# Feed-forward up products with both parts of the rows as one moving operand of 512 columns

## Chip, cores and metric

The kernel runs on one core of a Trainium2 chip. The metric is the device time of one execution in microseconds, lower is better. The engines are TensorE (PE in the profile; its weight loads are PEld), VectorE (DVE), ScalarE (ACT), GpSimd (POOL) and SyncE (SP), which issues the loads from HBM.

## What is computed

Two layers of a decoder trunk over 256 rows of 1024 features. Each layer has an attention part and a feed-forward part. Only the second changes:

```python
def conv_ffn(h, w_up, conv_w, conv_b, w_down):
    u = h @ w_up
    s = u.shape[1]
    up = jnp.pad(u, ((0, 0), (CONV_WIDTH - 1, 0), (0, 0)))
    c = conv_b
    for k in range(CONV_WIDTH):
        c = c + conv_w[k] * up[:, k:k + s]
    a, val = jnp.split(c, 2, axis=-1)
    return (jax.nn.gelu(a, approximate=True) * val) @ w_down
```

Here h is 256 x 1024 (the normalised rows), w_up is 1024 x 5632, the convolution runs over three neighbouring rows, and w_down is 2816 x 1024.

## The kernel before

All products are made from two parts of each operand, for precision: a high part that TensorE's fast 32-bit format holds exactly (`copy` on ScalarE rounds to it, L113) and a low part, the difference (`sub` on VectorE, L116). A product is then three matmuls: high by high, high by low, low by high (`mm3`, L375). Weights come through a stream (`Stream`, L145): each chunk of 512 KB is loaded into one of four `st` buffers, its high part is written into one of four `wh` buffers and its low part into one of four `wl` buffers. A chunk is requested two chunks ahead of its use (`next`, L198).

A scheduler orders the instructions of each engine from the program and a model of their times; every engine then runs its own queue in that order and waits on semaphores. A pool tag with several buffers is given out as they come free. PSUM has eight banks of 512 32-bit columns, two for each of the tags T, mm, S and O (`bank`, L92); accesses to one bank are kept in program order.

The feed-forward stage is `ffn_layer` (L992). The rows stand transposed in two tiles of 128 partitions x 8 slices x 256 rows: `hh` (high part) and `hl` (low part), tag `q8`, written by `t8` (L388) from `out_layer` (L950). There are 22 column groups j of 128 features, each with two halves (the gelu side and the value side):

- j = 0 and 1: `up_first` (L1055) makes them with the rows as stationary operand and 512 weight columns as moving one, and `up_first_T` (L1072) transposes the result into T banks.
- j = 2 to 21: `up(j, half)` (L1014) has the weights as stationary operand and the rows as moving one. For each of the 8 slices k there are three matmuls of 256 columns: `wh` with `hh` (L1022), `wh` with `hl` (L1023), `wl` with `hh` (L1024). All 24 accumulate into the same 256 columns of a bank; the two halves of a j lie side by side in one bank. The banks go T, T, mm, mm over four j.
- `act_gate(j, half)` (L1028), called after both halves: `conv` (L1004) reads the bank three times (ScalarE L1007, VectorE L1008 and L1009); then come the gelu (L1031), the product of the two halves (L1035) and its split into `gh` and `gl`.
- `down(j, t)` (L1041): `mm3` on two banks of 512 columns, 12 matmuls for both t. It runs two groups behind: a round is up of j (both halves), then down of j - 2. The last two j have their up products one after the other; eight down steps follow in a fixed order.

After the last down products of a row half, `post_norm` and, in layer 0, `gained` and `t8` make the rows for the next layer. Queries (`qA`, `qB`, `qR`, L549) and the branch outputs (`out_T`, L698) of the attention part use the same tag `q8`, three buffers of 8 KB per partition, and so does the first chunk of the up weights. The 128-column rows, the convolution results and `gh`, `gl` are tiles of tag `k1`, eleven buffers.

Of the kernel before, what the change touches and what calls it, by code (L numbers as in the profile page):

```python
# [16 lines left out]
P = 128  # L17
# [48 lines left out]
def tile_hybrid_trunk(  # L66
# [138 lines left out]
    TAGS = {"kB": 1, "sg": 2, "q8": 3}  # L205
# [225 lines left out]
    def attn_layer(l, xp, rs, gains, first):  # L431
# [117 lines left out]
        qA, qB, qR = big8("q8", 3), big8("q8", 3), big8("q8", 3)  # L549
# [148 lines left out]
        def out_T(br, g):  # L698
            if OT[br] is None:
                OT[br] = big8("q8", 3)  # L700
            bv = OB[br][g].rearrange("p (k c) -> p k c", k=2)
            ho = OT[br][:, g * 2:g * 2 + 2, :]
            copy(ho, bv)
            sub(OT[br][:, 4 + g * 2:6 + g * 2, :], bv, r32(ho))
# [243 lines left out]
        return yp  # L948

    def out_layer(l, yp, gains):  # L950
        gains["ffn_pre"] = gain_tile(ffn_pre_gain, l)
        res = [[bank("O"), bank("O")], [bank("S"), bank("S")]]
        hp = big8("q8", 3), big8("q8", 3)
# [35 lines left out]
        return hp  # L989


    def ffn_layer(l, hp, gains, last):  # L992
        hh, hl = hp
# [10 lines left out]
        def conv(b, jj, half):  # L1004
            c = k1()
            u = b[:, half * T:(half + 1) * T]
            act.activation(c, u, AF.Identity, bias=cb(l, jj), scale=cw(l, 2, jj))  # L1007
            dve.scalar_tensor_tensor(c[:, 1:T], u[:, 0:T - 1], cw(l, 1, jj), c[:, 1:T], ALU.mult, ALU.add)  # L1008
            dve.scalar_tensor_tensor(c[:, 2:T], u[:, 0:T - 2], cw(l, 0, jj), c[:, 2:T], ALU.mult, ALU.add)  # L1009
            return c  # L1010
# [3 lines left out]
        def up(j, half, c0, c1):  # L1014
            if j not in up_bank:
                up_bank[j] = bank("T" if j % 4 < 2 else "mm")
# [3 lines left out]
            o = up_bank[j][:, half * T + c0:half * T + c1]  # L1020
            for k in range(8):
                pe.matmul(o, wh[:, k, :], hh[:, k, c0:c1], start=(k == 0), stop=False, skip_group_check=True)  # L1022
                pe.matmul(o, wh[:, k, :], hl[:, k, c0:c1], start=False, stop=False, skip_group_check=True)  # L1023
                pe.matmul(o, wl[:, k, :], hh[:, k, c0:c1], start=False, stop=(k == 7), skip_group_check=True)  # L1024
# [3 lines left out]
        def act_gate(j, half):  # L1028
            if half == 0:
                ca = ga[j] = conv(up_bank[j], j, 0)  # L1030
# [3 lines left out]
            cv = conv(up_bank.pop(j), 22 + j, 1)  # L1034
# [52 lines left out]
        for j in range(2, NJ):  # L1087
            for half in range(2):
                part(lambda: up(j, half, 0, T))
# [96 lines left out]
    for l in range(DEPTH):  # L1186
        yp = attn_layer(l, xp, rs, gains, l == 0)
        hp = out_layer(l, yp, gains)
        xp, rs = ffn_layer(l, hp, gains, l == DEPTH - 1)
# [79 lines left out]
```

## Time and profile before

| | us |
|---|---|
| median of three runs | 783.96 |
| lowest, highest | 782.5, 784.26 |
| the profiled execution | 782.81 |
| its span, first to last instruction | 781.0 |

In a profile, busy time is that in which an engine had an instruction under way. Matmuls overlap: the duration shown for one is longer than the distance to the next, so their rate is read from start to start. Idle time is put down to what released the engine, as inferred from semaphores. Names in rows leave out buffer numbers: `q` is any tile of tag `q8`, `k` any tile of tag `k1`, `k2` or `k4`; `mm`, `T`, `S` and `O` are banks.

### The profile page before, as it was taken

The numbers are of one execution on the slowest core, as the hardware profiler recorded it, in microseconds if no ns is written. First come the engines' busy times: TensorE is split into PE (matmuls) and PEld (weight loads), VectorE is DVE, ScalarE is ACT, GpSimd is POOL, SyncE is SP. The second block draws the span as 40 slices with busy tenths as digits, with TensorE's granted clock in tenths as the row PEclk, the third lists the DMA queues.
The fourth block names the chain that finished last, engine by engine and source line by source line (L and its number), as shares of the span: only waits on it lengthen the run. The fifth ranks groups of instructions, "written<-read, shape, count | busy, mean of one in ns | idle before, by whom it ended". The sixth has DMA issues, their size and how long they took to land.

```text
span 781.0 us, 12886 instructions
## 1 busy us (share of the span) xinstructions
PE 759.2 (97%) x4742; PEld 676.8 (87%) x4742; DVE 613.1 (79%) x1188; ACT 495.4 (63%) x950; POOL 34.0 (4%) x60
## 2 busy tenths in 40 slices
PE   8999999999899999999989999999999999999996
PEld 6788898887799999999868889988878999999995
DVE  6899898686787777777787989985876877677775
ACT  6596986754665555565556969866465655566552
POOL 4300001000100000000010000010010000000000
PEclk9999999999999999999999999999999999999999
DMA  8624264465566565665545323644645556656731
GB/s 337 196 86 133 64 219 170 136 188 162 173 205 189 188 187 184 209 210 188 164 134 163 95 82 121 200 153 162 200 144 172 188 187 189 188 182 201 217 104 54
DMA packets 42346, 131.26 MB, mean 168 GB/s; under 512 B 5375, under 2 KB 5931, under 8 KB 42283
## 3 DMA queue, kind: packets, MB, share of 16 engines
q1 hardware_dynamic: 41707, 129.39, 52.0%
q10 hardware_dynamic: 576, 1.05, 0.4%
q8 instruction: 37, 0.61, 0.3%
q14 instruction: 26, 0.21, 0.1%
HBM read 129.37 MB, written 1.05 MB: 167 GB/s over the span
## 4 chain that ended last, share of the span: by engine, by line
PE 83%; ACT 8%; DVE 4%; POOL 2%; issue 1%; DMA 1%; SPq 0%; DVEq 0%; POOLq 0%; ACTq 0%
PE mm L376 6%; PE mm L378 6%; PE mm L377 6%; PE T L1024 5%; PE mm L1023 5%; PE T L1023 5%; PE mm L1024 5%; PE T L1022 5%; PE mm L1022 5%; PE S L377 5%; PE S L376 5%; PE S L378 5%; PE O L376 3%; PE O L377 3%; PE O L378 3%; ACT k L635 2%
## 5 line engine op out<-in xcount | busy, mean ns | idle before, releaser
L117 DVE TENSOR_TENSOR wl<-st,wh 128x1024 fp32r<-128x1024 f32 (+2 forms) x220 | 260.4, 1186 | 101.5 <-ACT wh L114 100.3
L114 ACT ACTIVATE wh<-st 128x1024 fp32r<-128x1024 f32 (+2 forms) x220 | 225.5, 1028 | 178.1 <-PE O L378 40.5
L376 PE MATMUL mm<-wh,x 128*128 128x512 f32 (+2 forms) x248 | 92.9, 375 | 0.7 <-DVE VT L546 0.6
L377 PE MATMUL mm<-wl,x 128*128 128x512 f32 (+2 forms) x248 | 91.6, 370 | 0.0
L378 PE MATMUL mm<-wh,x 128*128 128x512 f32 (+2 forms) x248 | 91.3, 368 | 0.1
L1023 PE MATMUL mm<-q,wh 128*128 128x256 f32 x320 | 90.7, 284 | 0.0
L1024 PE MATMUL T<-q,wl 128*128 128x256 f32 x320 | 90.6, 283 | 0.0
L1023 PE MATMUL T<-q,wh 128*128 128x256 f32 x320 | 90.6, 283 | 0.0
L1024 PE MATMUL mm<-q,wl 128*128 128x256 f32 x320 | 90.6, 283 | 0.0
L1022 PE MATMUL T<-q,wh 128*128 128x256 f32 x320 | 90.5, 283 | 0.0
L1022 PE MATMUL mm<-q,wh 128*128 128x256 f32 x320 | 90.5, 283 | 0.0
L1022 PEld LDWEIGHTS mm<-q,wh 128*128 128x128 f32 x320 | 61.4, 192 | 0.9
L1022 PEld LDWEIGHTS T<-q,wh 128*128 128x128 f32 x320 | 61.4, 192 | 0.8
L1023 PEld LDWEIGHTS mm<-q,wh 128*128 128x128 f32 x320 | 61.4, 192 | 0.8
L1023 PEld LDWEIGHTS T<-q,wh 128*128 128x128 f32 x320 | 61.4, 192 | 0.7
L1024 PEld LDWEIGHTS mm<-q,wl 128*128 128x128 f32 x320 | 61.4, 192 | 0.1
L1024 PEld LDWEIGHTS T<-q,wl 128*128 128x128 f32 x320 | 61.4, 192 | 0.0
L378 PEld LDWEIGHTS mm<-wh,x 128*128 128x128 f32 x248 | 46.7, 188 | 6.1 <-DVE x L117 0.5
L376 PEld LDWEIGHTS mm<-wh,x 128*128 128x128 f32 x248 | 46.7, 188 | 6.0 <-issue 0.8
L377 PEld LDWEIGHTS mm<-wl,x 128*128 128x128 f32 x248 | 46.7, 188 | 4.8
L635 ACT ACTIVATE k<-k,mn 128x128 f32<-128x128 f32 (+1 forms) x96 | 42.4, 445 | 7.1 <-DVE mn L632 7.0
L114 ACT ACTIVATE k<-k 128x256 fp32r<-128x256 f32 x72 | 29.1, 413 | 9.1 <-DVE k L1035 5.6
(294 smaller groups left out, 1657.0 us busy)
## 6 DMA issues: line engine op xcount, KB each, us to landing
st<-in_ffn_w_up_dram SPq DMA_DIRECT2D x88, 512.0 KB, 4.2
st<-in_ffn_w_down_dram SPq DMA_DIRECT2D x44, 512.0 KB, 3.9
st<-in_w_in_dram SPq DMA_DIRECT2D x42, 512.0 KB, 3.6
st<-in_w_out_dram SPq DMA_DIRECT2D x16, 512.0 KB, 3.8
st<-in_w_in_dram SPq DMA_DIRECT2D x16, 384.0 KB, 3.1
st<-in_cmp_w_dram SPq DMA_DIRECT2D x16, 256.0 KB, 2.6
st<-in_w_branch_a_dram SPq DMA_DIRECT2D x8, 512.0 KB, 3.6
st<-in_w_branch_b_dram SPq DMA_DIRECT2D x8, 512.0 KB, 3.5
```

The costliest lines, as they stand in the source:

```text
L114: return act.activation(dst, src, AF.Copy, scale=scale)
L117: dve.tensor_tensor(dst, a, b, ALU.subtract)
L376: pe.matmul(o, xh, wh, start=first, stop=False, skip_group_check=True)
L377: pe.matmul(o, xh, wl, start=False, stop=False, skip_group_check=True)
L378: pe.matmul(o, xl, wh, start=False, stop=last, skip_group_check=True)
L635: last_exp[0] = act.activation(self.pt[:, hh, s, :], sm[:, :nk], AF.Exp, bias=self.mn[:, i:i + 1], scale=-1.0, accum_out=self.dn[:, i:i + 1])
L1022: pe.matmul(o, wh[:, k, :], hh[:, k, c0:c1], start=(k == 0), stop=False, skip_group_check=True)
L1023: pe.matmul(o, wh[:, k, :], hl[:, k, c0:c1], start=False, stop=False, skip_group_check=True)
L1024: pe.matmul(o, wl[:, k, :], hh[:, k, c0:c1], start=False, stop=(k == 7), skip_group_check=True)
```

## The change

The two parts of the rows now lie in one tile `H` of 128 partitions x 2 parts x 8 slices x 256 rows (tag `h16`, one buffer of 16 KB per partition). `H[:, 0]` and `H[:, 1]` serve in turn as `qA` and `qB`, as the branch outputs, and as `hh` and `hl`; tag `q8` keeps one buffer, for `qR` and the first chunk of the up weights.

For j from 2 on, a slice k is two matmuls: `wh` with both parts of the rows as one moving operand of 512 columns, which fills a whole bank (left half: with the high part, right half: with the low part), and `wl` with the high part, 256 columns, added to the left half. Each half of a j has a bank of its own, mm for even j and T for odd j. Before the convolution, `left` copies the right half of the bank to SBUF on ScalarE and adds the left half on VectorE; the convolution then reads the sum from SBUF. The first two j are as before.

```diff
-    TAGS = {"kB": 1, "sg": 2, "q8": 3}
+    TAGS = {"kB": 1, "sg": 2, "q8": 1}
...
-        qA, qB, qR = big8("q8", 3), big8("q8", 3), big8("q8", 3)
+
+        H = ap_.tile([P, 2, KD, T], F32R, tag="h16", name=nm("H"))
+        qA, qB, qR = H[:, 0], H[:, 1], big8("q8", 1)
...
-                OT[br] = big8("q8", 3)
+                OT[br] = H[:, br]
...
-        hp = big8("q8", 3), big8("q8", 3)
+        hp = H[:, 0], H[:, 1]
...
-        def conv(b, jj, half):
+        def conv(u, l_, jj):
             c = k1()
-            u = b[:, half * T:(half + 1) * T]
...
-        def up(j, half, c0, c1):
-            if j not in up_bank:
-                up_bank[j] = bank("T" if j % 4 < 2 else "mm")
+
+        def up(j, half):
+            b = up_bank[j, half] = bank("mm" if j % 2 == 0 else "T")
             if (j, half) not in up_w:
                 up_w[j, half] = W.next(8, P)
             wh, wl, _ = up_w[j, half]
-            o = up_bank[j][:, half * T + c0:half * T + c1]
+            both = b.rearrange("p (s t) -> p s t", s=2)
             for k in range(8):
-                pe.matmul(o, wh[:, k, :], hh[:, k, c0:c1], start=(k == 0), stop=False, skip_group_check=True)
-                pe.matmul(o, wh[:, k, :], hl[:, k, c0:c1], start=False, stop=False, skip_group_check=True)
-                pe.matmul(o, wl[:, k, :], hh[:, k, c0:c1], start=False, stop=(k == 7), skip_group_check=True)
+                pe.matmul(both, wh[:, k, :], H[:, :, k, :], start=(k == 0), stop=False, skip_group_check=True)
+                pe.matmul(b[:, 0:T], wl[:, k, :], hh[:, k, :], start=False, stop=(k == 7), skip_group_check=True)
+
+        def left(j, half):
+            if j < 2:
+                return up_bank[j][:, half * T:(half + 1) * T]
+            b = up_bank.pop((j, half))
+            u = k1()
+            copy(u, b[:, T:2 * T])
+            dve.tensor_tensor(u, b[:, 0:T], u, ALU.add)
+            return u
...
-                ca = ga[j] = conv(up_bank[j], j, 0)
+                ca = ga[j] = conv(left(j, 0), l, j)
...
-            cv = conv(up_bank.pop(j), 22 + j, 1)
+            cv = conv(left(j, 1), l, 22 + j)
```

## Rows read from the trace of the kernel before

**Rows 1.** The page: busy us, share of the span, instructions of each engine.
```profile
PE 759.2 (97%) x4742; PEld 676.8 (87%) x4742; DVE 613.1 (79%) x1188; ACT 495.4 (63%) x950; POOL 34.0 (4%) x60
```
**Rows 2.** Busy us by stretch; columns as in the first line.
```profile
core 0: us, PE busy (x) PEld busy (x) DVE busy (x) ACT busy (x) POOL busy (x), PEclk, DMA share, GB/s
...
239.26:358.64 119.38, 119.38 (x842) 112.14 (x840) 88.72 (x129) 68.06 (x100) 0.00 (x0) 1.00 0.62 195
...
624.00:743.38 119.38, 119.38 (x842) 112.14 (x840) 88.74 (x129) 68.29 (x100) 0.00 (x0) 1.00 0.63 194
```
**Rows 3.** Longest of PE's waits from 206 to 400: total us, times, longest.
```profile
PE T L383 <- DVE k L415: 2.9, 2, 1.6
```
**Rows 4.** PE in order of time, one round: start us, duration us, line, operation.
```profile
281.90 0.28 PE L1022 MATMUL mm<-q,wh 128*128 128x256 f32 x1
...
287.53 0.28 PE L1024 MATMUL mm<-q,wl 128*128 128x256 f32 x1
287.65 0.39 PE L376 MATMUL S<-wh,k 128*128 128x512 f32 x1
...
290.42 0.28 PE L1022 MATMUL mm<-q,wh 128*128 128x256 f32 x1
```
**Rows 5.** PE in time: third input tile (41 us), first up products (200 us).
```profile
41.53 0.40 PE L376 MATMUL mm<-wh,x 128*128 128x512 f32 x1
...
43.13 0.39 PE L377 MATMUL mm<-wl,x 128*128 128x512 f32 x1
...
200.72 0.39 PE L376 MATMUL mm<-wh,q 128*128 128x512 f32 x1
...
204.58 0.39 PE L378 MATMUL mm<-wh,q 128*128 128x512 f32 x1
```
**Rows 6.** PE in time: eight matmuls of 32 columns, and the next.
```profile
133.41 0.96 PE L825 MATMUL S<-kcs,q 128*128 128x32 f32 x8
134.22 0.48 PE L376 MATMUL mm<-wh,x 128*128 128x512 f32 x1
```
**Rows 7.** Groups from 239.26 to 358.64: busy us, mean ns | idle before, releaser.
```profile
L117 DVE TENSOR_TENSOR wl<-st,wh 128x1024 fp32r<-128x1024 f32 x42 | 51.4, 1224 | 25.0 <-ACT wh L114 24.8
L1008 DVE SCALAR_TENSOR_TENSOR k<-T,vec,k 128x255 f32<-128x255 f32 x16 | 7.6, 477 | 0.0
L1035 DVE TENSOR_TENSOR k<-k,k 128x256 f32<-128x256 f32 x14 | 6.0, 425 | 0.5
...
L114 ACT ACTIVATE wh<-st 128x1024 fp32r<-128x1024 f32 x42 | 44.2, 1058 | 43.4 <-PE O L378 16.3 <-PE T L1023 13.7 <-PE mm L1023 13.4
```
**Rows 8.** Groups by form, whole execution, columns as above.
```profile
L114 ACT ACTIVATE k<-mm,rstd 128x256 f32<-128x256 f32 x8 | 3.3, 467 | 0.0
L407 DVE SCALAR_TENSOR_TENSOR X<-k,rstd,X 128x512 f32<-128x512 f32 x16 | 11.4, 747 | 1.7 <-POOL rstd L365 1.7
L490 DVE SCALAR_TENSOR_TENSOR k<-mm,rstd,tab 128x512 f32<-128x512 f32 x4 | 3.0, 747 | 1.6 <-POOL tab L358 1.6
```
**Rows 9.** ACT and DVE in time: a weight chunk's two parts, with idle time before.
```profile
279.20 1.06 ACT L114 ACTIVATE wh<-st 128x1024 fp32r<-128x1024 f32 x1 [1.49 <-PE T L1023]
...
280.30 1.23 DVE L117 TENSOR_TENSOR wl<-st,wh 128x1024 fp32r<-128x1024 f32 x1 [1.32 <-ACT wh L114]
```
**Rows 10.** DVE and PE in time: last read of a T bank, second half of j = 3.
```profile
224.43 0.48 DVE L1009 SCALAR_TENSOR_TENSOR k<-T,vec,k 128x254 f32<-128x254 f32 x1
...
226.52 0.28 PE L1022 MATMUL mm<-q,wh 128*128 128x256 f32 x1
```
**Rows 11.** In time, end of layer 0's stage: last up matmul, convolutions, low part.
```profile
378.56 0.28 PE L1024 MATMUL T<-q,wl 128*128 128x256 f32 x1
...
380.03 0.55 ACT L1007 ACTIVATE k<-T,vec 128x256 f32<-128x256 f32 x1
...
382.74 0.55 ACT L1007 ACTIVATE k<-T,vec 128x256 f32<-128x256 f32 x1
...
386.68 0.42 DVE L117 TENSOR_TENSOR k<-k,k 128x256 fp32r<-128x256 f32 x1
```

More of the change, by code (lines that the diff above doesn't have):

```diff
@@ L947, in attn_layer, with out_layer @@
         branch(1)
-        return yp
-    def out_layer(l, yp, gains):
+        return yp, H
+    def out_layer(l, yp, H, gains):
         gains["ffn_pre"] = gain_tile(ffn_pre_gain, l)
         res = [[bank("O"), bank("O")], [bank("S"), bank("S")]]
-        hp = big8("q8", 3), big8("q8", 3)
+        hp = H[:, 0], H[:, 1]
         ch = {}
@@ L988, in out_layer, with ffn_layer @@
                 W.make()
-        return hp
-    def ffn_layer(l, hp, gains, last):
-        hh, hl = hp
+    def ffn_layer(l, H, gains, last):
+        hh, hl = H[:, 0], H[:, 1]
         gains["ffn_post"] = gain_tile(ffn_post_gain, l)
@@ L1002, in down_bank @@
             return banks[t]
-        def conv(b, jj, half):
+        def conv(u, l_, jj):
             c = k1()
-            u = b[:, half * T:(half + 1) * T]
-            act.activation(c, u, AF.Identity, bias=cb(l, jj), scale=cw(l, 2, jj))
-            dve.scalar_tensor_tensor(c[:, 1:T], u[:, 0:T - 1], cw(l, 1, jj), c[:, 1:T], ALU.mult, ALU.add)
-            dve.scalar_tensor_tensor(c[:, 2:T], u[:, 0:T - 2], cw(l, 0, jj), c[:, 2:T], ALU.mult, ALU.add)
+            act.activation(c, u, AF.Identity, bias=cb(l_, jj), scale=cw(l_, 2, jj))
+            dve.scalar_tensor_tensor(c[:, 1:T], u[:, 0:T - 1], cw(l_, 1, jj), c[:, 1:T], ALU.mult, ALU.add)
+            dve.scalar_tensor_tensor(c[:, 2:T], u[:, 0:T - 2], cw(l_, 0, jj), c[:, 2:T], ALU.mult, ALU.add)
             return c
         up_bank, up_w, gs, wdn = {}, {}, {}, {}
-        def up(j, half, c0, c1):
-            if j not in up_bank:
-                up_bank[j] = bank("T" if j % 4 < 2 else "mm")
+        def up(j, half):
+            b = up_bank[j, half] = bank("mm" if j % 2 == 0 else "T")
             if (j, half) not in up_w:
@@ L1088, in ffn_layer @@
             for half in range(2):
-                part(lambda: up(j, half, 0, T))
+                part(lambda: up(j, half))
             for half in range(2):
@@ L1186, in tile_hybrid_trunk @@
     for l in range(DEPTH):
-        yp = attn_layer(l, xp, rs, gains, l == 0)
-        hp = out_layer(l, yp, gains)
-        xp, rs = ffn_layer(l, hp, gains, l == DEPTH - 1)
+        yp, H = attn_layer(l, xp, rs, gains, l == 0)
+        out_layer(l, yp, H, gains)
+        xp, rs = ffn_layer(l, H, gains, l == DEPTH - 1)
     idle(50)
```

## The prediction

> **What bounds the kernel now.** I read the busy times of the page first: TensorE (PE) is busy 97% of the span, VectorE (DVE) 79%, ScalarE 63% [rows 1]. A busy PE need not be a PE that sets the end, so next I read the busy time by stretch, for the feed-forward stage of each layer, the only stage whose products change. From 239.26 to 358.64 us of layer 0, fourteen equal rounds, PE is busy for all 119.38 us, and just as long in layer 1; DVE is busy 88.72 us of it (74%), ScalarE 68.06 us (57%), the DMA share is 0.62, and the granted clock 1.00 [rows 2], which is the 2.4 GHz level. So in this stage each nanosecond taken from a matmul is a nanosecond of the result, as long as no other engine comes late. PE never waits in these rounds; its one long wait of the stage is 2.9 us at layer 0's end [rows 3].
>
> The third view is PE in order of time, for the distance from one start to the next, since the durations shown overlap. One round is two up products of 24 matmuls with 256 columns each, then twelve down matmuls with 512 columns. The 48 narrow ones start from 281.90 to 287.65 us: 5.75/48 = 0.1198 us apart. The twelve wide ones go from 287.65 to 290.42: 2.77/12 = 0.2308 us [rows 4]. In the first products of the stage, which also use 512 columns, 17 starts go from 200.72 to 204.58, 0.2271 us apart [rows 5]. At 2.4 GHz 256 columns need 0.1067 us and 512 need 0.2133 us, so a matmul pays some 13 to 17 ns beyond its columns, and nearly the same whether it is narrow or wide. That fixed part is what the change can save.
>
> **The change part by part.** *The matmuls.* Per 128-row slice k of an up product, before has three matmuls of 256 columns (wh with hh, wh with hl, wl with hh): 3 x 0.1198 = 0.3594 us. After has one of 512 (wh with hh and hl) and one of 256 (wl with hh): between 0.2271 + 0.1198 = 0.3469 and 0.2308 + 0.1198 = 0.3506 us. The saving is 8.8 to 12.5 ns; I take the middle, 10.7 ns. There are 2 layers x 20 j x 2 halves x 8 slices = 640 of them: 5.6 to 8.0 us, 6.8 us taken. The columns that stream stay the same; 640 of 4742 matmuls and their weight loads go.
>
> Two things could spoil that price. The 512 columns lie in two pieces 8 KB apart. The trace has such an operand: the third input tile reads its weights in four pieces of 128 columns, and its starts go from 41.53 to 43.13 us in seven steps, 0.2286 us each [rows 5]. So pieces cost nothing. And the weights of the wide matmul must load while only 256 columns stream. Eight matmuls of 32 columns, each with its own weights, take from 133.41 to 134.22 us, 0.101 us each [rows 6], which bounds a load from above; it is under the 0.12 us that are there.
>
> Here a rule speaks against the change. The Trainium skill, TensorE: Matmul & The Clock Gate, section Back-to-back issue gap, gives N/2.4 + 2.5 ns for the gap of isolated warm matmuls, a fixed part of 2.5 ns and not of 13. By it a merged pair would save 2.5 ns, and the sum would be 1.6 us instead of 6.8. The rows differ, and I follow the rows.
>
> *The handover.* Each half of each j from 2 on (80 in all) gains a ScalarE copy of the right half of its bank and a DVE addition. The copy's nearest row is the copy of 256 columns from PSUM at 467 ns; the addition's is the SBUF multiplication of 256 columns at 425 ns, and PSUM as a source makes no difference on DVE (747 ns from SBUF, 747 ns from PSUM for 512 columns) [rows 7, 8]. Per round that adds 0.93 us to ScalarE and 0.85 us to DVE. The round itself shrinks from 8.53 us to 8.53 - 16 x 0.0107 = 8.36. DVE goes from 88.72/14 = 6.34 to 7.19 us of 8.36 (86%), ScalarE from 4.86 to 5.79 us (69%). Both stay under the round, so I cost them at nothing: their cover is the PE's own work.
>
> What has to hold for that: the DVE addition now stands between the matmul and the convolution, in DVE's queue, behind the splitting of weights (wl, 1.22 us) that itself waits for ScalarE. Queued behind the addition are the two convolution steps, the gate product and the next wl; waiting for these are the down product of j (two rounds later, some 17 us) and the next up products. A weight buffer is refilled as soon as PE lets go of it: the copy starts at 279.20, the wl from 280.30 is done at 281.53 [rows 9], and with four buffers the chunk is wanted three chunks later, 8.5 us after the release. So 6 us of slack. The PSUM banks: after the change j and j+1 use all four, so the banks of j must be read before j+2 begins, a round later, and now after the copy and the addition alone. No wait comes from that in the steady rounds.
>
> *The start of the stage.* j = 3 now takes the T banks in which the first two j stand transposed. The last read of those ends at 224.91 us; the second half of j = 3 starts at 226.52 [rows 10]. It fits with 1.6 us to spare: cost 0, at most the 0.9 us of two handovers per layer if ScalarE or DVE come late there, 1.8 us for both.
>
> *The end of layer 0's stage.* Before, both halves of a j share a bank, so the convolution of the last j's first half starts only when the second is complete: up ends at 378.68, the two convolutions start at 380.03 and 382.74, the gate's low part at 386.68 us [rows 11]. After it PE waits 2.9 us in all for the normalised rows of the next layer [rows 3]. With a bank for each half, the first could start 2.9 us sooner, but the chain of each gains a copy and an addition (0.89 us), and for the last two j, four up products with no down product between them, DVE has four wl and two handovers: 4 x 1.22 + 2 x 3.6 = 12.1 us in 11.2 us. I take 0; the bounds are a gain of the whole 2.9 us and a loss of 1.8 us (two handovers).
>
> *The tiles.* q and k for attention, the branch outputs and the rows of the feed-forward layer share one 16 KB tile in place of three of 8 KB in rotation. The same buffers are free long before they are written again, since the writers come after the last reader in program order either way: 0.
>
> The sum: 782.81 us for the profiled execution (span 781.0 and 1.8 around it), less 6.8, is 776.0. The median of the three runs, 783.96, is 1.15 us above that execution; on its scale 777.2 us. I predict 777.0.
>
> **The rivals.**
> 1. *The merged matmul saves nothing.* If the part beyond the columns went with the columns and not with the instruction, or if two pieces 8 KB apart cost what four near ones don't, a wide matmul here would take twice the narrow one's 0.1198 us, 0.2396, and the time stays at 784.0. For it: no row shows this very operand. Against it: 0.1198 and 0.2271 to 0.2308 us are means over many starts, and 0.2396 is above both of the latter. The skill's rule named above comes near this case; it would give 782.4, and its case is counted here.
> 2. *The ends of the stage eat a part.* 6.8 us less up to 1.8 at the starts and 1.8 at layer 0's end: 780.8. For it: DVE is over its time in the last two j. Against it: the first half of each j is free sooner.
> 3. *The handover becomes the bound, slower.* DVE's idle time in a round, (119.38 - 88.72)/14 = 2.19 us, is nearly all spent in front of wl, waiting for ScalarE's copy: 25.0 us over the fourteen rounds, 1.79 each [rows 7]. If the orders of the two queues hold these waits fixed, a round lasts 8.53 + 0.85 = 9.38 us. That would decide after the 6 us of slack in the weights, that is after about 6 of the 20 rounds (1.02 us lag in each): 14 rounds x 0.85 x 2 layers = 24 us more, 6 x 0.17 x 2 = 2 us less: 806 us. Against it: ScalarE's copy waits for PE itself (43.4 us before wh, all released by PE [rows 7]), so it comes early and the waits are spare time which shrinks when DVE comes later.
>
> **How the numbers follow.** The forecast, 773 to 779.5 us, has 0.74; rival 1 0.06; rival 2 0.11; rival 3 0.09. Low end: 783.96 - 8.0 - 2.9 = 773.1, rounded down to 772.5 for the lower profiled execution. High end: rival 2 at 780.8, with 0.2 for the spread. This leaves out rivals 1 and 3, 0.15. A change of 0.2% (1.6 us) is what a measurement here can tell from none. Faster by that: the forecast and rival 2, 0.85; within it: rival 1, 0.06; slower: rival 3, 0.09.
>
> **What would show it.** In the profile after: up matmuls as 640 of 512 and 640 of 256 columns, with 0.347 to 0.351 us from one wide start to the next; rounds of 8.3 to 8.4 us; PE still busy for all of a round; DVE near 86% and its idle time before wl down to about 1 us a round. Wrong would be: PE idle before an up product with a DVE addition or a wl as its releaser (rival 3), a wide matmul of 0.24 us or more (rival 1), or a longer wait at the transposes at the end of layer 0 (rival 2).

## The result: the products got shorter, the kernel got slower

The changed kernel takes 791.72 us (median; 789.88 to 792.25), the kernel before, on the same chip, 784.11 (782.5 to 784.93). The ratio is 1.0099, with a 95% interval of 1.0084 to 1.0113: 7.6 us lost where 7 were to be won. The profiled execution of the changed kernel took 789.88 us with a span of 788.1, which is 7.1 more than the 781.0 before.

First the page, busy us, share of the span and instructions of each engine, against [rows 1]:

```profile
PE 756.3 (96%) x4102; PEld 641.3 (81%) x4102; DVE 637.8 (81%) x1268; ACT 523.3 (66%) x1030; POOL 34.5 (4%) x60
```

The 640 matmuls are gone, and VectorE and ScalarE have 80 instructions more each. Then the fourteen rounds of layer 0 in the changed kernel, columns as in [rows 2]:

```profile
239.26:358.64 119.38, 118.78 (x623) 100.74 (x623) 97.71 (x159) 78.35 (x129) 0.00 (x0) 1.00 0.58 195
```

PE is still busy nearly all the time, at the same clock, and neither of the other two is near its limit: VectorE 82%, ScalarE 66%. So the page and the stretch show no reason for a loss. PE in order of time, the two up products of j = 10 and the start of the down product behind it (start us, duration us), shows the gain, against [rows 4]:

```profile
281.29 0.40 PE L1022 MATMUL mm<-H,wh 128*128 128x512 f32 x1
...
286.73 0.28 PE L1023 MATMUL mm<-H,wl 128*128 128x256 f32 x1
286.84 0.39 PE L376 MATMUL S<-wh,k 128*128 128x512 f32 x1
```

Sixteen pairs from 281.29 to 286.84 are 0.3469 us each, where three narrow matmuls took 0.3594. A steady round is 8.385 us (down products start at 244.96 and 312.03, eight rounds apart), not 8.53. The loss must lie elsewhere, and the list of PE's waits from 206 to 400 us (total, times, longest) says where, against the 2.9 us of [rows 3]:

```profile
PE S L376 <- ACT k L114: 5.0, 4, 3.8
PE T L383 <- DVE k L415: 3.3, 2, 2.0
PE T L1022 <- DVE k L1009: 0.5, 1, 0.5
```

The first line is new: a down product that waits for `gh`, ScalarE's high part of the gate. Its longest wait stands at the end of the layer, in time (the wait and its releaser in brackets):

```profile
386.97 0.79 PE L376 MATMUL S<-kB,k 128*128 128x512 f32 x1 [3.84 <-ACT k L114]
387.57 0.63 PE L377 MATMUL S<-kB,k 128*128 128x512 f32 x1
```

A ledger of the spans, from the first matmul behind the last up product and the first matmul behind the stage:

| | before | after | change |
|---|---|---|---|
| layer 0, behind the ups | 378.68 | 377.85 | -0.8 |
| next layer's first matmul | 394.01 | 399.31 | +5.3, so the end lost 6.1 |
| layer 1, behind the ups | 763.42 | 767.91 | +4.5, so -0.8 again |
| end of span | 781.0 | 788.1 | +7.1, so the end lost 2.6 |

The ends lose 8.7 us, the rounds win 1.6. At equal work both are larger, 9.6 and 2.5: in each layer of the changed kernel two down matmuls, 0.47 us, run ahead of the last up product and count here to the rounds:

```profile
371.91 0.40 PE L377 MATMUL S<-wl,k 128*128 128x512 f32 x1
372.15 0.45 PE L1022 MATMUL T<-H,wh 128*128 128x512 f32 x1
...
377.85 0.39 PE L378 MATMUL S<-wh,k 128*128 128x512 f32 x1
```

Why the ends? The gate is late, and has been late since the start of the stage. To see it, take the start of a gate's last step, `gl` on VectorE, and the start of the down product of the same j that reads it; the distance I call the margin. In the kernel before, for j = 2, 3, 4 (pairs of `gl` and down start, VectorE and PE in time):

```profile
233.17 0.42 DVE L117 TENSOR_TENSOR k<-k,k 128x256 fp32r<-128x256 f32 x1
236.49 0.39 PE L376 MATMUL S<-wh,k 128*128 128x512 f32 x1
...
238.81 0.42 DVE L117 TENSOR_TENSOR k<-k,k 128x256 fp32r<-128x256 f32 x1
245.02 0.39 PE L376 MATMUL S<-wh,k 128*128 128x512 f32 x1
...
244.45 0.42 DVE L117 TENSOR_TENSOR k<-k,k 128x256 fp32r<-128x256 f32 x1
253.54 0.39 PE L376 MATMUL S<-wh,k 128*128 128x512 f32 x1
```

The margin is 3.3, 6.2, 9.1 us: the stage begins with a backlog, since the gates of j = 0 and 1 come together, and the kernel before works it off at 8.53 - 5.64 = 2.9 us a round; from then on the margin is 9.1 (8.2 at the least, around two early weight conversions). The same pairs in the changed kernel, j = 2, j = 8 and j = 17:

```profile
236.09 0.42 DVE L117 TENSOR_TENSOR k<-k,k 128x256 fp32r<-128x256 f32 x1
236.54 0.39 PE L376 MATMUL S<-wh,k 128*128 128x512 f32 x1
...
286.39 0.42 DVE L117 TENSOR_TENSOR k<-k,k 128x256 fp32r<-128x256 f32 x1
286.84 0.39 PE L376 MATMUL S<-wh,k 128*128 128x512 f32 x1
...
362.82 0.42 DVE L117 TENSOR_TENSOR k<-k,k 128x256 fp32r<-128x256 f32 x1
363.33 0.39 PE L376 MATMUL S<-wh,k 128*128 128x512 f32 x1
```

0.45, 0.45 and 0.51 us: the backlog is never worked off. A gate takes exactly a round, 8.36 to 8.41 us from `gl` to `gl`. As long as rounds follow, that costs nothing but two waits of 0.3 us around these two early conversions (called at j = 14 and 16), which make four rounds 1.0 us longer (34.54 us from 312.03 to 346.57, steady ones 33.54). At the end there is no round left to hide in: `gl` of j = 20 and 21 start at 386.95 and 391.89, 9.1 and 14.0 us after the ups, where in the kernel before they came 2.3 and 8.0 us after them.

What keeps the gate there is seen in ScalarE's queue, in time, one round of the changed kernel (idle time before an instruction in brackets):

```profile
284.15 1.06 ACT L114 ACTIVATE wh<-st 128x1024 fp32r<-128x1024 f32 x1 [0.80 <-PE mm L1022]
285.21 0.42 ACT L114 ACTIVATE k<-k 128x256 fp32r<-128x256 f32 x1
285.54 0.37 ACT L114 ACTIVATE k<-T 128x256 f32<-128x256 f32 x1
286.92 1.06 ACT L114 ACTIVATE wh<-st 128x1024 fp32r<-128x1024 f32 x1 [1.01 <-PE mm L1022]
287.89 0.59 ACT L1007 ACTIVATE k<-k,vec 128x256 f32<-128x256 f32 x1
288.38 0.36 ACT L114 ACTIVATE k<-T 128x256 f32<-128x256 f32 x1
289.82 1.06 ACT L114 ACTIVATE wh<-st 128x1024 fp32r<-128x1024 f32 x1 [1.07 <-PE O L378]
```

At 285.54 it copies out of a T bank, the product of j = 9, while PE is already at the end of j = 10. The copy could run far earlier, but it stands in the queue behind weight conversions (`wh`), and each of these waits for PE to let a weight buffer go. PE releases one every 2.8 us, three a round. So conversions tick at PE's pace, and the gate's steps stand between them: copy, conversion, convolution and copy, conversion, and so on. As long as each conversion waits for PE, a gate spread over three of them takes a round, whatever the engines have to spare. In the kernel before, two conversions stand between one gate and the next as long as it is late (four `wh` from 233.17 to 244.45, two gates), and three once it is on time (six from 244.45 to 261.51).

### The profile page after: what moved, and what is told of

The parts are those of the page before. It is cut to its first block, busy times and chain, and to the rows that moved or that the text cites. A ratio compares the mean times of both kernels' runs of the same rounds, so it can differ in the third digit from the quotient of the medians.

```text
span 788.1 us, 11893 instructions
## 1 busy us (share of the span) xinstructions
PE 756.3 (96%) x4102; PEld 641.3 (81%) x4102; DVE 637.8 (81%) x1268; ACT 523.3 (66%) x1030; POOL 34.5 (4%) x60
## 4 chain that ended last, share of the span: by engine, by line
PE 77%; ACT 9%; DVE 8%; POOL 2%; issue 2%; DMA 1%; DVEq 0%; SPq 0%; ACTq 0%
PE T L1022 9%; PE mm L1022 8%; PE mm L376 6%; PE mm L378 6%; PE mm L377 6%; PE S L376 5%; PE T L1023 5%; PE S L377 5%; PE S L378 5%; PE mm L1023 4%; PE O L377 3%; PE O L376 3%; PE O L378 3%; DVE wl L117 3%; ACT wh L114 2%; PE T L664 2%
## 5 line engine op out<-in xcount | busy, mean ns | idle before, releaser
L1022 PE MATMUL T<-H,wh 128*128 128x512 f32 x320 | 113.1, 396 | 0.9 <-DVE k L1009 0.9
L1022 PE MATMUL mm<-H,wh 128*128 128x512 f32 x320 | 112.9, 394 | 0.0
L1023 PE MATMUL mm<-H,wl 128*128 128x256 f32 x320 | 89.7, 280 | 0.0
L1023 PE MATMUL T<-H,wl 128*128 128x256 f32 x320 | 89.4, 279 | 0.0
L1022 PEld LDWEIGHTS T<-H,wh 128*128 128x128 f32 x320 | 60.0, 187 | 16.0 <-issue 1.5
L1022 PEld LDWEIGHTS mm<-H,wh 128*128 128x128 f32 x320 | 60.0, 187 | 13.8
L1023 PEld LDWEIGHTS mm<-H,wl 128*128 128x128 f32 x320 | 60.5, 189 | 0.9
L1023 PEld LDWEIGHTS T<-H,wl 128*128 128x128 f32 x320 | 60.3, 189 | 0.8
L1007 ACT ACTIVATE k<-k,vec 128x256 f32<-128x256 f32 x80 | 47.2, 590 | 12.9 <-DVE k L1031 12.9
L1008 DVE SCALAR_TENSOR_TENSOR k<-k,vec,k 128x255 f32<-128x255 f32 x80 | 38.4, 479 | 6.8 <-ACT k L1007 6.8
```

Of the source, the lines that this page charges most:

```text
L1007: act.activation(c, u, AF.Identity, bias=cb(l_, jj), scale=cw(l_, 2, jj))
L1008: dve.scalar_tensor_tensor(c[:, 1:T], u[:, 0:T - 1], cw(l_, 1, jj), c[:, 1:T], ALU.mult, ALU.add)
L1022: pe.matmul(both, wh[:, k, :], H[:, :, k, :], start=(k == 0), stop=False, skip_group_check=True)
L1023: pe.matmul(b[:, 0:T], wl[:, k, :], hh[:, k, :], start=False, stop=(k == 7), skip_group_check=True)
```

## Experiments

All edits are against the changed kernel unless another is named; times are medians, ratios are against the kernel before on the same chip, with 95% intervals. e2, e7, e8 and e9 leave a part of the result out, the others nothing.

| run | us | ratio | margin at j = 8, 17 |
|---|---|---|---|
| before | 784.11 | 1 | 9.1, 9.1 |
| after | 791.72 | 1.0084 to 1.0113 | 0.45, 0.5 |
| e1_tiles_only | 783.86 | 0.9993 to 1.0016 | 9.1, 9.1 |
| e2_no_handover | 776.84 | 0.9894 to 0.9924 | 11.5, 11.6 |
| e3_last_two_narrow | 786.80 | 1.0025 to 1.0053 | 0.45, 0.45 |
| e4_hand_order | 787.25 | 1.0031 to 1.0075 | 10.7, 9.8 |
| e5_narrow_from_16 | 779.74 | 0.9942 to 0.9970 | 0.45, 6.2 |
| e6_one_half | 788.97 | 1.0050 to 1.0094 | 2.35, 2.35 |
| e7_copy_only | 777.03 | 0.9901 to 0.9935 | 11.5, 11.6 |
| e8_vector_only | 785.79 | 1.0018 to 1.0042 | 0.5, 0.5 |
| e9_off_chain | 778.02 | 0.9906 to 0.9942 | 11.5, 11.5 |
| e10_start_narrow | 785.81 | 1.0015 to 1.0039 | 11.25, 6.0 |
| e11_hand_4_20 | 791.96 | 1.0093 to 1.0123 | 10.75, 9.65 |
| e12_hand_narrow_20 | 787.73 | 1.0035 to 1.0068 | 10.5, 9.7 |
| e13_first_tap_vector | 789.44 | 1.0050 to 1.0097 | 0.4, 0.4 |
| e14_tap_narrow_20 | 786.61 | 1.0020 to 1.0046 | 0.5, 0.4 |
| e15_tap_on_left | 785.97 | 1.0020 to 1.0045 | 0.4, 3.2 |
| e16_start_narrow_moved | 781.28 | 0.9951 to 0.9977 | 11.3, 11.2 |
| e17_wide_6_to_20 | 781.42 | 0.9969 to 0.9991 | 11.2, 11.2 |
| e18_before_moved | 784.93 | 1.0003 to 1.0027 | 9.1, 9.1 |

**Which part of the change.** The tile `H` alone, with the three narrow matmuls of before (against the kernel before; what only passes `H` on is left out here):

```diff
-        qA, qB, qR = big8("q8", 3), big8("q8", 3), big8("q8", 3)
+        H = ap_.tile([P, 2, KD, T], F32R, tag="h16", name=nm("H"))
+        qA, qB, qR = H[:, 0], H[:, 1], big8("q8", 1)
...
-                OT[br] = big8("q8", 3)
+                OT[br] = H[:, br]
...
-        hp = big8("q8", 3), big8("q8", 3)
+        hp = H[:, 0], H[:, 1]
```

> The shared tile H and the single q8 buffer of the change, with the three matmuls of 256 columns, the banks and the convolution of the kernel before. Theory A (the handover, copy and addition, stands a round late in the queues of ScalarE and VectorE, and the end of each layer pays for it) and theory B (ScalarE and VectorE have no time for the handover in a round) expect 784 us, the time of before, within 1 us. Theory C (the shared tile makes writers wait) expects 788 to 792.

783.86 us: the shared tile costs nothing. Next, the wide matmuls without the handover:

```diff
-            u = k1()
-            copy(u, b[:, T:2 * T])
-            dve.tensor_tensor(u, b[:, 0:T], u, ALU.add)
-            return u
+            return b[:, 0:T]
```

> The changed kernel without copy and addition: the convolution reads the left half of the bank directly, so the product of the weights' high part with the rows' low part, which stands in the right half, is left out of the result. All matmuls stay. Theories A and B expect the gain of the matmuls without its price: 776 to 779 us, rounds of 8.36 us, and the wait at layer 0's end no longer than before (3 us in all). Theory C, and any theory by which two banks for a j are the trouble, expects 786 or more.

776.84 us, and in the fourteen rounds (columns as in [rows 2])

```profile
239.26:358.64 119.38, 119.38 (x629) 101.87 (x628) 91.01 (x134) 69.69 (x103) 0.00 (x0) 1.00 0.61 198
```

The products are worth what was forecast, and the handover alone costs 791.7 - 776.8 = 14.9 us, twice what they save.

**Where it is paid.** The handover was then left out where a layer ends:

```diff
+                if j >= NJ - 2:
+                    pe.matmul(b[:, 0:T], wh[:, k, :], hh[:, k, :], start=(k == 0), stop=False, skip_group_check=True)
+                    pe.matmul(b[:, 0:T], wh[:, k, :], hl[:, k, :], start=False, stop=False, skip_group_check=True)
+                else:
                     pe.matmul(both, wh[:, k, :], H[:, :, k, :], start=(k == 0), stop=False, skip_group_check=True)
...
             b = up_bank.pop((j, half))
+            if j >= NJ - 2:
+                return b[:, 0:T]
```

> The changed kernel, with three matmuls of 256 columns and no handover for the last two j (20 and 21) alone, so that the chain behind the last up product is as short as in before. If the loss sits only in the chain of the last two j (2 x about 4 us: two handovers each and ScalarE and VectorE waiting for one another), 780 us or less. If the loss is the lateness of a whole round that all j carry to the end (theory A or B), the late gates of j = 18 and 19 remain in front of those of 20 and 21, and the time stays above 785.

786.8 us: 4.9 us of the 14.9 come back, no more, for the two rounds inherit a gate that is a round late (margin 0.45 at j = 17). With more rounds (both conditions of e3):

```diff
-                if j >= NJ - 2:
+                if j >= 16:
```

> The last six j of each layer (16 to 21) take the three narrow products and no handover; j = 2 to 15 are as in the changed kernel. Nothing of the result is left out. The theory that the handover costs nothing in the rounds and is paid only where a gate runs a round late into the end of a layer: the six rounds without handover drain the lateness, as the rounds of the kernel before do, gl of the last j comes 0 to 1 us after its products as in the kernel before, the first matmul of the next layer starts 2 to 3 us before the 394.0 us of the kernel before, and the time is 784.1 less 28 rounds of 0.18 us, 779.0 (778 to 780.5). The rival that the rounds themselves lose (two engines that have no room with the handover, a lateness larger than six rounds can drain): 782 to 787, with a wait of the down products still standing in the last rounds.

779.74 us, faster than both kernels with nothing left out. The pairs of `gl` and down start for j = 15, 16, 17 show the backlog going as soon as the handover stops:

```profile
345.93 0.42 DVE L117 TENSOR_TENSOR k<-k,k 128x256 fp32r<-128x256 f32 x1
346.50 0.39 PE L376 MATMUL S<-wh,k 128*128 128x512 f32 x1
...
351.70 0.42 DVE L117 TENSOR_TENSOR k<-k,k 128x256 fp32r<-128x256 f32 x1
355.02 0.39 PE L376 MATMUL S<-wh,k 128*128 128x512 f32 x1
...
357.34 0.42 DVE L117 TENSOR_TENSOR k<-k,k 128x256 fp32r<-128x256 f32 x1
363.55 0.39 PE L376 MATMUL S<-wh,k 128*128 128x512 f32 x1
```

0.6, 3.3, 6.2 us: the same steps as at the start of the kernel before. No wait for `gh` is left at the end of layer 0; the 0.3 us in the list stand at 320.95, in the round of an early conversion:

```profile
PE T L383 <- DVE k L415: 1.6, 2, 1.2
PE T L1026 <- DVE k L1009: 0.5, 1, 0.5
PE S L376 <- ACT k L114: 0.3, 1, 0.3
```

So fourteen wide rounds a layer, all of them a round late, lose nothing themselves. The price is at the end, for a backlog not worked off.

**Engine time, or order.** Half the handovers, in the same two conditions:

```diff
-                if j >= NJ - 2:
+                if half == 1:
```

> Only the first half of each j is made as one wide product with a handover; the second half has the three narrow products. Nothing is left out. The product part saves half, 3.6 us. If the price of the handover goes with its number (a dose), it is half of 14.9 us, and the time 784.1 - 3.6 + 7.5 = 788. If it has a threshold (the gate catches up as long as the work of a round on the two engines and their waits for one another fits into 8.45 us), the backlog of the start drains, only slower than in the kernel before, and the time is 780.5 (779.5 to 782).

788.97 us, about what a price for each handover gives (788). But it isn't time on the engines that is paid for, as the fourteen rounds show:

```profile
239.26:358.64 119.38, 119.38 (x734) 106.91 (x733) 91.51 (x145) 72.28 (x115) 0.00 (x0) 1.00 0.63 196
```

VectorE has 91.51 us of work there, half a us more than in the run without handover, which works its backlog off and is 12 us faster; here a gate takes 8.47 us, a round, again. Now the two halves of the handover, one at a time. ScalarE's copy alone:

```diff
             copy(u, b[:, T:2 * T])
-            dve.tensor_tensor(u, b[:, 0:T], u, ALU.add)
```

> As the changed kernel, but without the add on VectorE: the gate reads ScalarE's copy of the right half, so the left half is left out of the result. It holds the ScalarE part of the handover and one crossing between engines fewer. If the lateness comes from where the copy stands in ScalarE's queue (behind the weight conversions, which wait for TensorE), most of the 14.9 us stays: 788 to 791. If it is VectorE's time (425 ns each, 0.85 us a round), most goes: 777 to 780.

777.03 us. VectorE's operation alone:

```diff
-            copy(u, b[:, T:2 * T])
-            dve.tensor_tensor(u, b[:, 0:T], u, ALU.add)
+            dve.tensor_copy(u, b[:, 0:T])
```

> As the changed kernel, but without ScalarE's copy: VectorE copies the left half to the tile that the gate reads, so the right half is left out of the result. It holds VectorE's part of the handover alone. If the price is VectorE's time, most of the 14.9 us stays: 788 to 791. If it is the copy's place in ScalarE's queue, most goes: 777 to 780. If neither of this run and the run with the copy alone shows over half of it, it is the crossing from the one to the other that costs, both being needed.

785.79 us. The copy is free (0.2 us), VectorE's operation is not: 8.9 of the 14.9 us. The other 5.8 come only with both together; no run takes them apart. In e8 `gl` of j = 20 and 21 start at 383.44 and 388.74, 3.5 and 3.2 us sooner than in the changed kernel. VectorE's time, or its place? The same number of VectorE operations, off the chain:

```diff
             copy(u, b[:, T:2 * T])
-            dve.tensor_tensor(u, b[:, 0:T], u, ALU.add)
+            dve.tensor_copy(k1(), b[:, 0:T])
             return u
```

> As the changed kernel, but the gate reads ScalarE's copy of the right half, and VectorE's operation on the left half has the same place in the source, 256 columns out of the same bank, and writes a tile that nobody reads: the left half is left out of the result. VectorE issues as many operations as in the changed kernel; only the step from ScalarE over VectorE back to ScalarE is gone from the head of the gate. If VectorE's time is the price, 786 to 791, like the run with VectorE's operation alone (785.8). If the price is the order that the step forces on the two queues, the gate catches up in the rounds (steps of gl under 8 us until it does, by j = 14 or so) and the time is 777 to 779.5, near the 777.0 of the run with the copy alone.

778.02 us. The fourteen rounds with VectorE's operation on the chain (e8):

```profile
239.26:358.64 119.38, 119.38 (x628) 101.85 (x628) 96.45 (x161) 69.95 (x102) 0.00 (x0) 1.00 0.61 197
```

and off it (e9), where both engines have more to do:

```profile
239.26:358.64 119.38, 119.38 (x628) 101.90 (x628) 101.01 (x167) 82.50 (x136) 0.00 (x0) 1.00 0.61 197
```

The operation takes the same time in both, 418 ns. With 101.01 us of VectorE work in 119.38, more than the changed kernel's 97.71, the run is 13.7 us faster than the changed kernel, as its gate works the backlog off: its pair for j = 8,

```profile
275.36 0.42 DVE L117 TENSOR_TENSOR k<-k,k 128x256 fp32r<-128x256 f32 x1
286.85 0.39 PE L376 MATMUL S<-wh,k 128*128 128x512 f32 x1
```

has a margin of 11.5 us, that of e8 0.5. In e8 twelve conversions stand in four steps from gate to gate (236.25 to 269.78), in e9 fifteen in six (233.43 to 275.36): three a gate against two and a half. VectorE's time by itself is thereby out as the cause: it is the operation's place on the chain, and with it the number of PE's ticks that a gate is spread over.

**Another order for the same work.** If order is the cause, a better one must help. Here ScalarE's and VectorE's instructions were put in program order for j = 2 to 21, copy and add right behind the up product, product and split a half later:

```diff
+        with tc.manual_schedule(engines=MANUAL1):
+            last_j = None
+            for j in range(2, NJ):
+                if last_j:
+                    product(*last_j)
+                part(lambda: up(j, 0))
+                if last_j:
+                    split(*last_j[:2])
+                u0 = src(j, 0)
+                part(lambda: up(j, 1))
+                c0 = conv(*u0)
+                u1 = src(j, 1)
+                gelu(c0)
...
+                c1 = conv(*u1)
...
```

> The changed kernel with the same instructions, but ScalarE and VectorE in an order written by hand from j = 2 on: copy and addition of a half stand right behind the up product that fills its bank, ahead of the next weight chunk, and the gate of a j is done within a round after its up products. Theory A (the order alone keeps the handover late) expects no wait of 0.4 us or more before the down products, a stall at layer 0's end near that of before, and 777 to 781 us. Theory B (no time in a round, whatever the order) expects rounds above 8.5 us or the same stalls at the ends: 788 or more.

787.25 us, between the two ranges. In the rounds it did a part of what was wanted: the margin grows from 8.6 us at j = 2 to 10.7 at j = 8, with a gate every 7.95 us. But it wasn't the full backlog that was worked off: the edit also reorders the gates of j = 0 and 1, so that `gl` of j = 1 starts at 222.80 (changed kernel 227.74), and the down product of j = 2 starts 2.5 us later. From 237.9 to 253.8 us there are three conversions a gate, and none of them waits for PE; the two engines wait for each other. This order leaves 0.4 us a round to win back; whether another leaves more is not shown. And it lost elsewhere: PE waited 2.5 us a layer for `wh` and `wl` at the start, and 3.9 us for the transposes at the end of layer 0, where the last gate stood behind conversions. Behind the start's waits in layer 1 the granted clock was 0.50 from 615.8 to 622.5 us, and the stage took 2.8 us longer than in layer 0. Twice more, for j = 4 to 19 only, the second time (e12) with the last two j narrow:

```diff
+HAND = (4, 20)
...
+            if j == HAND[0]:
+                with tc.manual_schedule(engines=MANUAL1):
+                    hand_rounds(range(*HAND))
+            if HAND[0] <= j < HAND[1]:
+                continue
```

```diff
+                if j >= 20:
+                    pe.matmul(b[:, 0:T], wh[:, k, :], hh[:, k, :], start=(k == 0), stop=False, skip_group_check=True)
+                    pe.matmul(b[:, 0:T], wh[:, k, :], hl[:, k, :], start=False, stop=False, skip_group_check=True)
...
+            if j >= 20:
+                return b[:, 0:T]
```

> All of the changed kernel's work, the order on ScalarE and VectorE written by hand for j = 4 to 19, left to the planner before and after; nothing is left out. The hand order of all j (787.3) drained the lateness in the rounds and lost time at the start, in two rounds and at the end. If the order is the cause, gl steps under 8.36 us again drain it, the start's loss of 2.5 us a layer goes, and the time is 781 to 785. If engine time is the cause, 788 to 792.

> As the run with hand order for j = 4 to 19, and the last two j with the three narrow products and no handover. Nothing is left out; 18 wide rounds a layer, 6.5 us of product time less than the kernel before. If order is the cause and the end is then that of the kernel before, 777.5 to 780; if the four weight conversions that stand ahead of j = 20 in ScalarE's queue hold up the last gates, 781 to 784.

791.96 us, in the range set for engine time as the cause, and 787.73, above both ranges. At the two seams, where my order meets the scheduler's (the planner of the expectations), 8.5 us lie between `gl` of j = 3 and 4, and 12.4 us between those of j = 18 and 19; at the second, four conversions stand ahead of `gh` of j = 19 in ScalarE's queue. In the rounds between, the margin starts at 9.5 (e11) and 8.7 us (e12) and grows to 10.7. So the three hand-written orders show that the whole handover can be done in the rounds without the gate falling late; that a better order works a full backlog off, or makes the kernel faster, they don't show.

**A theory that didn't hold.** After e9 I held ScalarE's wait for the add, at the head of the gate, to be what spreads it. Two ways to keep the whole computation without that wait: the first tap of the filter on VectorE (e14: but for the last two j, which are narrow, by the conditions of e12),

```diff
+            if jj % 22 < 2:
+                act.activation(c, u, AF.Identity, bias=cb(l_, jj), scale=cw(l_, 2, jj))
+            else:
+                dve.tensor_scalar(c, u, cw(l_, 2, jj), cb(l_, jj), ALU.mult, ALU.add)
```

> The changed kernel with the first tap of the filter (u times a weight, plus the bias) on VectorE for j of 2 and more, in place of ScalarE. Nothing is left out. A half's gate then goes from ScalarE's copy to VectorE once, and not over to VectorE, back to ScalarE and to VectorE again; VectorE has one more operation a half (0.2 to 0.45 us, so 0.4 to 0.9 us more a round on top of 86% busy), ScalarE one fewer. If the order forced by that step is the cause, gl drains below 8.36 us a step and the time is 777.5 to 781. If VectorE's time is the cause, it is worse than the changed kernel: 791 to 800. If the planner still sets three conversions a j from the start, gl stays a round late and it is 786 to 790.

> As the run with the first tap on VectorE, and the last two j with the three narrow products, no handover and the tap on ScalarE. Nothing is left out. If the lateness drains in the rounds: 777 to 780; if not, as the run with only the last two narrow, 785 to 788.

and the first tap on ScalarE from the left half alone, with the right half's share added on VectorE:

```diff
+            else:
+                b, u = u, k1()
+                act.activation(c, b[:, 0:T], AF.Identity, bias=cb(l_, jj), scale=cw(l_, 2, jj))
+                copy(u, b[:, T:2 * T])
+                dve.scalar_tensor_tensor(c, u, cw(l_, 2, jj), c, ALU.mult, ALU.add)
+                dve.tensor_tensor(u, b[:, 0:T], u, ALU.add)
```

> The changed kernel with ScalarE's first tap made straight from the left half in the bank, its copy of the right half behind that, and on VectorE one more multiply-add that adds the right half's share of the tap, then the add. Nothing is left out. ScalarE has the work of the changed kernel and waits for no add; VectorE has 0.48 us more a half, 0.95 us a round, which makes 81.8 + 11.4 = 98% of the round with the 97.7 us per 119.4 us of the changed kernel and the 13.5 us more. If the step over VectorE is the cause and VectorE's time is not, 778 to 783; if VectorE's time becomes the bound there, rounds over 8.4 us and 790 to 800.

789.44, 786.61 and 785.97 us: margins of 0.4 to 0.5 us at j = 8 in all three. So taking that wait out is not enough. It isn't cleared either: both ways give VectorE more to do (108.42 us in e13 and 106.49 in e15 over the fourteen rounds, 101.01 in e9), and none was tried that doesn't. All runs with one more VectorE step in the chain, in any position, stay late when the planner orders them (after, e6, e8, e13, e14, e15; of these e15 alone wins something back, 2.7 us from j = 12 on); those without one work the backlog off (e2, e7, e9). What the planner weighs when it spreads a longer chain over one more conversion no trace shows; that is left open.

**Does a gate on time stay on time?** The handover left out at the start instead (both conditions of e3):

```diff
-                if j >= NJ - 2:
+                if j < 8:
```

> j = 2 to 7 take the three narrow products and no handover, j = 8 to 21 are as in the changed kernel: 14 wide rounds, as in the run whose last six were narrow (779.7), but the last gates of the layer carry the handover. Nothing is left out. If the lateness is only the backlog of the start that never drains, the first six rounds drain it at 5.64 us a step, the wide rounds keep time, and the ends pay only the last gates' own handover, 1 to 2 us a layer: 781 to 783. If the wide rounds lose the time again once something holds them up (the two rounds with an early conversion), the ends pay as in the changed kernel: 786 to 789.

785.81 us, which looked like an answer of no. The pairs for j = 12 and j = 17:

```profile
309.77 0.42 DVE L117 TENSOR_TENSOR k<-k,k 128x256 fp32r<-128x256 f32 x1
321.03 0.39 PE L376 MATMUL S<-wh,k 128*128 128x512 f32 x1
...
356.88 0.42 DVE L117 TENSOR_TENSOR k<-k,k 128x256 fp32r<-128x256 f32 x1
362.91 0.39 PE L376 MATMUL S<-wh,k 128*128 128x512 f32 x1
```

The margin holds at 11.3 us up to j = 12 and falls to 6.0 by j = 17, just over the rounds of the two early conversions. So these were moved into the narrow rounds (e16, and e18 for the kernel before):

```diff
-            if j in (NJ - 8, NJ - 6):
-                W.make(early[l, NJ - 1 if j == NJ - 6 else NJ - 2])
+            if j in (4, 6):
+                W.make(early[l, NJ - 1 if j == 6 else NJ - 2])
```

> As the run with j = 2 to 7 narrow (785.8), with the two early conversions of down weights moved from j = 14 and 16 to j = 4 and 6. Nothing is left out; 14 wide rounds a layer with the whole handover, to the end of the layer. If the handover costs nothing once the gate is on time, gl stays a whole round ahead of its use through all 14 rounds, and the time is 784.0 less 28 times 0.18, 779, plus 0 to 2.5 for the last gates' own handover: 779 to 781.5. If the handover itself makes the gate late again, 784 to 787 as without the move.

> The kernel before with the two early conversions at j = 4 and 6 and nothing else changed: what the move alone is worth. If the move only keeps the order of the wide rounds, 783 to 785; if it is worth time by itself, as much must be taken off what the run with the narrow start gained by it: 780 to 782.

781.28 us, and for the kernel before with the same move 784.93, no gain. In e16 the pair for j = 17,

```profile
351.99 0.42 DVE L117 TENSOR_TENSOR k<-k,k 128x256 fp32r<-128x256 f32 x1
363.18 0.39 PE L376 MATMUL S<-wh,k 128*128 128x512 f32 x1
```

still has 11.2 us: ten wide rounds with the whole handover (j = 8 to 17) keep time once the gate is on time. Last, more wide rounds (narrow for j = 2 to 5 and j = 21; against e16):

```diff
-                if j < 8:
+                if not 6 <= j < 21:
...
-            if j in (4, 6):
-                W.make(early[l, NJ - 1 if j == 6 else NJ - 2])
+            if j in (3, 5):
+                W.make(early[l, NJ - 1 if j == 5 else NJ - 2])
```

> Wide products and handover for j = 6 to 20, narrow ones for j = 2 to 5 and for the last j, the two early conversions at j = 3 and 5. Nothing is left out; 15 wide rounds a layer. If a gate that starts on time stays on time: 784.0 - 30 x 0.18 = 778.6 and little at the ends, 778 to 780. If four narrow rounds are too few to drain the start (8 us of lateness at 2.9 us a round), the lateness stays: 784 to 787.

781.42 us, over the 778 to 780 expected: the margin holds, but PE waits 1.9 us a layer at the start for a T bank (0.4 in e16), where the gates of j = 0 and 1 end later than in e16 (`gl` of j = 1 at 228.92 us, there at 227.92).

## Why the prediction was wrong, step by step

*What bounds the kernel.* Right for the rounds: PE is the bound, busy 118.78 of 119.38 us. (The "one long wait" of 2.9 us in [rows 3] is two waits, of 1.6 and 1.3.) But the ends of the stage are bounded by the gate, and by where it stands when the last up product is done; the prediction looked at each end as it was, not at what it inherits.

*The matmuls.* Right. The round shrank by 0.143 us (e2: 8.384, before 8.527), so 9 ns for each of the 640 pairs, 5.7 us, in the forecast's 5.6 to 8.0 and somewhat under the 6.8 taken; e2's 7.1 us (by its ratio) hold some 1.1 from a shorter wait at the end of layer 0 (1.8 in place of 2.9 us). A wide start costs 0.2325 us and the narrow one behind it 0.1165 (means over the fourteen rounds). Rival 1 fell. The Trainium skill, TensorE: Matmul & The Clock Gate, section Back-to-back issue gap, gives N/2.4 + 2.5 ns for isolated warm matmuls. An estimate from it is 1.6 us; the 5.7 measured in this stream decide against it.

*The handover, at nothing.* Here it failed: it cost 14.9 us (e2). Its sizes were good: 0.37 us for the copy (0.467 taken), 0.42 for the add (0.425), VectorE at 82% (86%), its idle time before `wl` at 17.2 us in place of 25.0 [rows 7], 1.2 us a round. The words "their cover is the PE's own work" hold as well, and just for the rounds. What the step left out is that a share below 100% does not tell how fast a late queue can catch up. Before, that rate was 2.9 us a round, after it was zero, with 18% of VectorE idle. The prediction asked who waits for the addition within a round, found slack, and didn't ask where the slack had come from: the 9.1 us of margin were won in the first three rounds. So nearly all its signs of being right are in the trace: the rounds, PE's busy time, VectorE's share and idle time. None of its signs of being wrong named the wait that came, a down product behind `gh`.

*Rival 3* had the mechanism half right, "if the orders of the two queues hold these waits fixed". It put the price on the length of a round (9.38 us) and on the weights. The rounds stayed at 8.385; the order held the gate at one a round and no more. That the kernel got slower had 0.09, by another wait and at 806 us.

*The start, 0 to 1.8 us.* Inside its bounds: PE waits 0.5 us a layer for a T bank, not at the second half of j = 3, which the working looked at, but at the first (219.79 us).

*The end of layer 0, -2.9 to +1.8 us.* Wrong: +6.1, outside its bounds. It is 3.84 and 0.52 us of waiting for `gh`, 0.4 more at the transposes, and 1.5 for seven slow matmuls (below): 6.3 of the 6.6 at equal work. The end of layer 1, +2.6, wasn't costed at all. *The tiles, 0.* Right (e1).

So the sum had its gain right and its sign wrong. In the spans of the profiled executions, less 5.7 for the products and 8.7 more at the ends make 3.0 of the 7.1 us; the other 4.1 are in the rounds: 0.9 for the T bank, 2.0 around the early conversions, 0.9 for the down matmuls that moved ahead, and 0.3 not accounted for.

## What to carry to other kernels

Before adding a step to a chain that runs beside a bound engine, read not only the busy shares but the margin, round by round from the start: how late the chain begins, how much it wins back a round, and how many instructions in its queues wait for the bound engine between two of its steps. If a longer chain wins nothing back, the price comes where the rounds end. A cheap cure is to go back to the old form early enough for the backlog to be worked off before the rounds end (e5, 779.74 us, in place of 784.11), or to start with it (e16, 781.28) and keep other extra work of those queues out of the new form's rounds.

## What the runs showed of the hardware

After PE's wait of 3.84 us at the end of layer 0 the granted clock fell to 0.50, the 1.2 GHz level (changed kernel, by stretch, columns as in [rows 2]; before the wait, behind it, and once it had risen again):

```profile
379.00:382.70 3.70, 3.70 (x17) 3.02 (x16) 2.77 (x5) 2.07 (x4) 0.00 (x0) 1.00 0.79 265
...
387.00:389.60 2.60, 2.60 (x6) 2.12 (x7) 1.92 (x5) 1.43 (x4) 0.00 (x0) 0.50 0.58 202
390.10:391.20 1.10, 1.10 (x6) 0.73 (x4) 0.96 (x3) 0.04 (x1) 0.00 (x0) 1.00 0.00 0
```

Seven matmuls of 512 columns, from 386.97 to 390.07, took 3.10 us, where seven at 0.233 take 1.63: the wait cost 1.5 us beyond itself. In the kernel before, the waits of 1.58 and 1.27 us at the transposes left the clock at 1.00 in the profiled execution. That is not so each time: in e18, with waits of 1.59 and 1.27 us at the same place, it was 0.50 behind them:

```profile
392.60:399.20 6.60, 5.72 (x16) 4.66 (x17) 5.42 (x9) 3.23 (x9) 2.17 (x6) 0.50 0.24 81
```

The next layer's attention part, from its first matmul to the up product of j = 2, then took 205.77 us in place of 203.84. The times on record go with it: executions of the kernel before near 782.4 us have a mean granted clock of 0.998, those near 785.2 one of 0.995, and three of the changed kernel's four have 0.990 or 0.991, the profiled one 0.996. So the price of a late gate includes the clock behind the wait. In the profiled execution of e8 the attention part behind the wait took 205.80 us, so about 2 of its 8.9 us are the clock; how much of the 14.9 us it makes no trace shows.

And a matmul's weights load beside the one ahead of it even when that streams only 256 columns: the narrow-to-wide distance is 0.1165 us, no longer than the 0.1198 of narrow to narrow [rows 4].
